# A hybrid decoder block on one core: the MLP's VectorE, ScalarE and TensorE instructions issued in the written order, and the sums of activations at places of their own

## The chip, the cores and the metric

One core of one Trainium2 chip runs the whole program. The time is the device time of one launch in microseconds (us), from an execution without the profiler; the median of several runs is compared. Engines are named as in the profile: PE is TensorE (PEld its weight loads), DVE is VectorE, ACT is ScalarE, POOL is GpSimd, SP issues most of the DMAs.

## The reference, cut to what matters

512 tokens with 16 meta tokens ahead of them pass through a mixer (a Mamba-2 part and an S5 part, one input and one output projection) and then through an MLP. All data are float32. The change touches the MLP and the step into it:

```python
m = _rmsnorm(h, g_mlp[layer]) @ w_up[layer]          # 512 x 1024 @ 1024 x 4096
h = h + jnp.square(jax.nn.relu(m)) @ w_down[layer]   # 512 x 4096 @ 4096 x 1024
return _rmsnorm(h, g_final)[:, N_META:]
```

## The kernel before

**Three matmuls for one.** Float32 operands are split into a high part (`whi`, `ah`: a cast to fp32r on ACT, line 1012) and a rest (`wlo`, `al`: the difference, on DVE, line 997), and each product is made as high x high, rest x high and high x rest.

**Seven products for eight.** Each matrix product of the MLP is done on 2 x 2 blocks with seven block products in place of eight (a Strassen-like scheme). So sums of blocks are needed on both sides, of weights and of tokens, and sums of products behind them.

**Quarters, groups, steps.** The 4096 hidden columns go in four quarters of 1024, each of two groups of 512. A quarter has 28 steps, numbered 0 to 27 within it and 0 to 111 over all (`for i in range(112)`, line 1394):

- Steps 0 to 13 are the up projection (`up`, line 1217): seven products P1 to P7 for each of the two groups, 24 matmuls of 128 x 256 each. In quarters 1 to 3 the order is P1, P5, P6, P2, P7, P3, P4 of group 0, then of group 1; quarter 0 has an order of its own (line 1153).
- Steps 14 to 27 are the down projection (`down`, line 1254): products n = 0 to 6 (`PRODUCTS`), each for group 0 and group 1, 12 matmuls of 128 x 512 each. The last product is done for both groups at once in step 27 (`last`).

**Taking over an up product** (lines 1236 to 1252). The products of a group go to three PSUM banks, X (P1, P6, P7, P4), Y (P2) and Z (P5, P3). P1, P5 and P6 are copied into the tile `r` by ACT. P2, P7 and P3 are added to or subtracted from what is in `r` by DVE, and ACT then applies relu and square (lines 1073 and 1074). P4 goes through relu and square on ACT alone. A bank that is used again must have been taken over first. The pool of these banks (tag `u`) has six.

**Weights.** `Cols` and `Rows` load blocks of `w_up` and `w_down` with SP (lines 1052 and 1091) and form sums of them: `s1` (two DVE additions, line 99), `s2` (one), `s4` (a DMA issued by POOL that adds while it writes, line 1009), and `t1`, `t2`, `t4` for the rows. The loads and the sums have due steps in the table `self.at`; `ahead(i)` does what is due at step i. In quarters 1 to 3, `s1` is due one step ahead of a group's first product, `s2` at that product, `s4` one later. `split(i + 2)` casts and splits the weights for the step after next (three buffers each for `whi` and `wlo`), and for down steps the operand of activations (two buffers for `ah` and `al`).

**Sums of activations** (`Sums`, line 1110). The down products need S1 = a11 - a10, S2 = -(S1) - a00, S3 = a00 - a10 and S4 = -(S2) - a01 of blocks of `r`. `Sums.get` computes each at the moment that its product is split: S1 and S2 in `split` of step 18, S3 of step 22, S4 of step 24, each over both groups.

**The order.** The program is recorded in the order in which it is written, and a scheduler then makes a queue for each engine. It goes by priority (the written order, moved ahead by `tc.high_priority(offset=AHEAD)`) among what its own estimate of the times holds to be ready, so an engine's queue can differ from the written order. In each round of the loop the written order is `ahead(i)`, `split(i + 2)`, then `run(i)` with the take-over. Within a queue an engine goes in order.

**The step into the MLP.** Tokens come in four tiles of 128. Tiles 0 and 1 are transposed and split during the end of the output projection (`first_blocks`). Tiles 2 and 3 are done by `late_tokens` (line 1379), written behind step 0 at high priority: `turned` transposes (PE) into two PSUM banks, DVE makes two differences (t1, t2), ACT and DVE split them into `opB`, and ACT copies the transposed blocks into `H`. In steps 4, 5 and 7 three more operands (`opC`) are made from `H`. `TOK` says which operand a product uses: P1 and P2 `opA`, P5 and P6 `opB`, P7, P3 and P4 `opC`.

**The end.** In the last quarter the finished parts of the output rows are normed as they come (`finish`, line 1307, after products n = 1, 4, 5, and `last_half`, `last_done`).

## Time and profile before

| | us |
|---|---|
| median of 3 runs | 819.64 (818.76 to 822.69) |
| the profiled execution | 819.08 |
| its span, first to last instruction | 817.4 |
| mean granted clock of PE | 0.991 |
| first MLP matmul, last MLP matmul | 472.36, 809.2 |

The mixer takes the first 472 us, the MLP the rest. By engine, over the stretch 740 to 770 us (up steps) PE is busy all 30.0 us, DVE 23.6, ACT 21.9; over 770 to 800 us (down steps) PE 28.6, DVE 29.7, ACT 18.8.

How to read it: a row of a timeline has the start, the duration, the engine, the line, the operation, output <- inputs, the shapes, how many instructions were merged, and in brackets how long the engine had been idle and what released it. A group of the page has, behind its count, busy time and mean duration in ns, then the idle time of its engine just before it. A DVE operation of 128 x 1024 takes 1.22 us, and the next one starts 1.14 us after it; matmuls overlap in the same way, so their rate is read from a run of many.

### The profile page before, as it was taken

What the parts mean: (1) busy time and instruction counts of PE and PEld (TensorE: products, weight loads), DVE (VectorE), ACT (ScalarE), POOL (GpSimd) and SP (SyncE); (2) the same over time, 40 slices, a digit from 0 to 9 for tenths busy, and PEclk for the clock granted to TensorE, in tenths of its full rate; (3) what the DMA queues carried; (4) which work ended last, traced back from release to release, by engine and by line L of the source; (5) the groups of instructions that cost most, each with busy time, mean ns of one, the idle gap of its engine ahead of it and who ended that gap; (6) DMA issues with size and microseconds to landing.
All of it is one profiled execution on the core that took longest, in us unless ns stands there. A gap on an engine that the chain in (4) does not pass through costs nothing. (4 is left out here: it accounts for less than half of the span.)

```text
span 817.4 us, 12922 instructions
## 1 busy us (share of the span) xinstructions
PE 774.6 (95%) x4943; PEld 682.0 (83%) x4943; DVE 625.9 (77%) x972; ACT 496.3 (61%) x782; POOL 75.5 (9%) x125
## 2 busy tenths in 40 slices
PE   6999899999999999989999989999999999999996
PEld 6999898998787778768888879878997899789975
DVE  4489798998785779769534588698679867987897
ACT  7578798988544753555123475654665466546665
POOL 3211000011000110010100000100010001000101
PEclk9999999999999999999999999999999999999998
DMA  9999575768664654344335028864485448654622
GB/s 242 194 232 217 113 167 138 172 141 190 144 154 133 163 131 132 104 125 160 123 103 186 21 78 244 192 155 156 129 181 155 156 130 181 180 159 112 117 51 104
DMA packets 129638, 121.90 MB, mean 149 GB/s; under 512 B 21836, under 2 KB 105720, under 8 KB 129576
## 3 DMA queue, kind: packets, MB, share of 16 engines
q1 hardware_dynamic: 121224, 90.66, 37.7%
q0 software_dynamic: 8352, 30.41, 20.4%
q8 instruction: 39, 0.64, 0.3%
q14 instruction: 23, 0.19, 0.1%
HBM read 83.76 MB, written 6.88 MB: 111 GB/s over the span
## 5 line engine op out<-in xcount | busy, mean ns | idle before, releaser
L997 DVE TENSOR_TENSOR wlo<-quad,whi 128x1024 fp32r<-128x1024 f32 x40 | 49.0, 1224 | 37.1 <-ACT whi L1012 34.5
L1232 PE MATMUL u<-opC,whi 128*128 128x256 f32 x384 | 71.5, 288 | 3.0 <-DVE r L99 2.0
L1012 ACT CAST whi<-quad 128x1024 fp32r<-128x1024 f32 x40 | 41.9, 1048 | 49.3 <-DMA quad<-raw 17.3
L1273 PE MATMUL acc<-whi,al 128*128 128x512 f32 x160 | 63.4, 396 | 3.7 <-DVE al L997 3.7
L1232 PEld LDWEIGHTS u<-opC,whi 128*128 128x128 f32 x384 | 60.6, 195 | 4.6 <-DVE r L99 2.6
L117 ACT CAST whi<-raw 128x1024 fp32r<-128x1024 f32 x31 | 32.3, 1043 | 52.6 <-PE acc L837 31.6
L118 DVE TENSOR_TENSOR wlo<-raw,whi 128x1024 fp32r<-128x1024 f32 x31 | 37.9, 1222 | 31.8 <-ACT whi L117 31.2
L1273 PE MATMUL acc<-whi,ah 128*128 128x512 f32 x160 | 59.6, 393 | 1.4 <-ACT ah L1012 1.4
L1273 PE MATMUL acc<-wlo,ah 128*128 128x512 f32 x160 | 60.3, 390 | 0.0
L139 PE MATMUL pxb<-xhi,whi 128*128 128x264 f32 x192 | 55.3, 288 | 1.6 <-ACT xcr L695 1.6
L139 PE MATMUL pxb<-xhi,wlo 128*128 128x264 f32 x192 | 55.8, 291 | 0.0
L139 PE MATMUL pxb<-xlo,whi 128*128 128x264 f32 x192 | 55.5, 289 | 0.0
L1232 PE MATMUL u<-opC,wlo 128*128 128x256 f32 x192 | 54.0, 286 | 0.0
L1012 ACT CAST whi<-bquad 128x1024 fp32r<-128x1024 f32 x34 | 35.7, 1049 | 30.0 <-PE acc L1273 20.8
L1232 PE MATMUL u<-opB,whi 128*128 128x256 f32 x256 | 48.6, 288 | 1.2 <-DVE opB L997 1.2
L1232 PE MATMUL u<-opA,whi 128*128 128x256 f32 x256 | 46.7, 280 | 0.2 <-ACT whi L1012 0.2
L997 DVE TENSOR_TENSOR wlo<-bquad,whi 128x1024 fp32r<-128x1024 f32 x34 | 41.5, 1221 | 3.2 <-ACT whi L1012 3.2
L1232 PEld LDWEIGHTS u<-opB,whi 128*128 128x128 f32 x256 | 40.8, 194 | 1.6 <-DVE opB L997 1.4
L1273 PEld LDWEIGHTS acc<-whi,al 128*128 128x128 f32 x160 | 30.0, 188 | 13.4 <-DVE al L997 7.5
L1232 PEld LDWEIGHTS u<-opA,whi 128*128 128x128 f32 x256 | 39.5, 188 | 0.6 <-ACT whi L1012 0.4
L1232 PE MATMUL u<-opB,wlo 128*128 128x256 f32 x128 | 37.1, 290 | 2.4 <-DVE wlo L997 2.4
L122 POOL DMA_DIRECT2D wlo<-raw x26 | 22.3, 856 | 179.2 <-ACT xcr L695 62.0
(435 smaller groups left out, 2429.0 us busy)
## 6 DMA issues: line engine op xcount, KB each, us to landing
raw<-in_w_in_dram SPq DMA_DIRECT2D x28, 512.0 KB, 4.2
wlo<-raw POOLq DMA_DIRECT2D x26, 512.0 KB, 5.2
raw<-in_w_up_dram SPq DMA_DIRECT2D x22, 512.0 KB, 4.2
raw<-in_w_glu_dram SPq DMA_DIRECT2D x16, 512.0 KB, 4.0
raw<-in_w_out_dram SPq DMA_DIRECT2D x16, 512.0 KB, 4.2
bquad<-in_w_down_dram SPq DMA_DIRECT2D x16, 512.0 KB, 3.6
quads<-in_w_down_dram SPq DMA_DIRECT2D x16, 512.0 KB, 4.4
bquad<-quads POOLq DMA_DIRECT2D x16, 512.0 KB, 5.1
```

Of the source, the lines that this page charges most:

```text
L117: A.copy(hi, raw)
L118: V.tensor_tensor(out=lo, in0=raw, in1=hi.bitcast(F32), op=ALU.subtract)
L122: G.dma_start(out=lo.bitcast(F32), in_=raw, accum_op=ALU.add)
L139: T.matmul(ps_out, lhsT=w[a][:, k, 0:m], rhs=x[b][:, k, tok], start=(n == 0), stop=(n == len(steps) - 1))
L997: V.tensor_tensor(out=out, in0=a, in1=b, op=ALU.subtract)
L1012: A.copy(hi, src)
L1232: T.matmul(pb[:, mm], lhsT=w[a][:, k, mm * P:(mm + 1) * P], rhs=x[:, b, k], start=(first and n == 0), stop=(n in (11, 23)), skip_group_che ...
L1273: T.matmul(banks[s], lhsT=at[x][:, g, j, s * P:(s + 1) * P], rhs=wt[y][:, j], start=(fresh and g == 0 and j == 0 and k == 0), stop=(g == 1 ...
```

## The change

It does four things.

1. `V`, `A` and `T` become wrappers (`InOrder`). While `on` is set, each instruction issued through a wrapper is tied behind the one issued before it on that engine, in order of issue and with no wait for its end. It is switched on for all three ahead of step 0; at step 107 it is switched off for VectorE and ScalarE. POOL and SP are not wrapped, and neither is anything written before step 0.
2. The sums of activations leave `Sums.get` and become due steps of their own: S1 and S2 of group 0 at step 8 (12 in quarter 0), of group 1 at step 15, S3 at 19, S4 at 20.
3. `late_tokens` is cut into `late_sums`, `late_split` and `late_copies`, no longer at high priority, and steps 0 to 3 are written out with these parts between them.
4. In these first steps the splits of weights for steps 2 to 5 are put between the parts, `s2` of the first group stands behind step 1, and `ahead(1)` stands with `ahead(3)` behind step 2.

```diff
+class InOrder:
+    def __init__(self, tc, engine):
+        self.tc, self.engine, self.on, self.last = tc, engine, False, None
+    def __getattr__(self, name):
+        f = getattr(self.engine, name)
+        def issue(*args, **kwargs):
+            r = f(*args, **kwargs)
+            if self.on:
+                if self.last is not None:
+                    self.tc.add_manual_dep(
+                        r.ins, self.last.name,
+                        mybir.DependencyInfo(mybir.DependencyClass.NoSync, mybir.DependencyReason.DATA),
+                        reason="in order")
+                self.last = r.ins
+            return r
+        return issue
...
-    V, A, G, T = nc.vector, nc.scalar, nc.gpsimd, nc.tensor
+    V, A, G, T = InOrder(tc, nc.vector), InOrder(tc, nc.scalar), nc.gpsimd, InOrder(tc, nc.tensor)
...
+        def first(self, g):
+            a = self.a
+            sub(self.s1[:, g], a[1, 1][:, g], a[1, 0][:, g])
+            neg_sub(self.s2[:, g], self.s1[:, g], a[0, 0][:, g])
+        def third(self):
+            sub(self.s1, self.a[0, 0], self.a[1, 0])
+        def fourth(self):
+            neg_sub2(self.s2, self.s2, self.a[0, 1])
         def get(self, m):
-            a = self.a
             if m in ("11", "12", "22"):
-                return a[int(m[0]) - 1, int(m[1]) - 1]
-            if m == "S2":
-                sub(self.s1, a[1, 1], a[1, 0])
-                neg_sub2(self.s2, self.s1, a[0, 0])
-            elif m == "S3":
-                sub(self.s1, a[0, 0], a[1, 0])
-            elif m == "S4":
-                neg_sub2(self.s2, self.s2, a[0, 1])
+                return self.a[int(m[0]) - 1, int(m[1]) - 1]
             return self.s1 if m in ("S1", "S3") else self.s2
...
+            self.add(12 if q == 0 else 8, self.sums_first)
+            self.add(15, lambda: self.sums.first(1))
+            self.add(19, lambda: self.sums.third())
+            self.add(20, lambda: self.sums.fourth())
...
+        def sums_first(self):
+            self.sums = Sums(self.rs)
+            self.sums.first(0)
...
-                if i == 14:
-                    self.sums = Sums(self.rs)
...
-    def late_tokens(t):
+    def late_sums(t):
+        c = slice((t - 2) * P, (t - 1) * P)
+        t1 = H[:, 0, 0, :, c]
+        src = [turned(t, k) for k in range(2)]
+        sub(t1, src[0], t1)
+        sub(t2[:, :, c], src[1], t1)
+        return src
+    def late_split(t, o):
+        c = slice((t - 2) * P, (t - 1) * P)
+        split_into(opB[:, o, 0, :, c], opB[:, o, 1, :, c], H[:, 0, 0, :, c] if o else t2[:, :, c])
+    def late_copies(t, src):
         c = slice((t - 2) * P, (t - 1) * P)
         for k in range(2):
...
+            A.copy(H[:, k, 1, :, c], src[k])
...
-    for i in range(112):
+    for e in (V, A, T):
+        e.on = True
+    def run(i):
+        quarters[i // 28].run(i % 28)
+    run(0)
+    src2 = late_sums(2)
+    split(2)
+    src3 = late_sums(3)
+    for t in late:
+        late_split(t, 1)
+    split(3)
+    run(1)
+    quarters[0].cols[0].s2()
+    late_copies(2, src2)
+    late_copies(3, src3)
+    for t in late:
+        late_split(t, 0)
+    split(4)
+    run(2)
+    for i in range(1, 4):
+        if i != 2:
+            ahead(i)
+    split(5)
+    run(3)
+    for i in range(4, 112):
...
-        if i > 0:
-            ahead(i)
+        if i == 107:
+            V.on = A.on = False
+        ahead(i)
         split(i + 2)
...
-        quarters[i // 28].run(i % 28)
-        if i == 0:
-            with tc.high_priority(offset=AHEAD):
-                for t in late:
-                    late_tokens(t)
+        run(i)
```

## The prediction

> **What bounds the kernel now.** I read the page, then what TensorE (PE) waits for in the MLP, then its clock there, then the rows of each engine in time.

> ```profile
> span 817.4 us, 12922 instructions
> PE 774.6 (95%) x4943; PEld 682.0 (83%) x4943; DVE 625.9 (77%) x972; ACT 496.3 (61%) x782; POOL 75.5 (9%) x125
> ```

> PE is the bound. The MLP begins at 472.4 us, so a change there can only gain what PE loses there:

> ```profile
> PE acc L1273 <- DVE al L997: 3.7, 6, 0.7
> PE u L1232 <- DVE wlo L997: 2.8, 2, 2.4
> PE u L1232 <- DVE r L99: 2.0, 1, 2.0
> PE acc L1273 <- ACT ah L1012: 1.4, 1, 1.4
> PE u L1232 <- DVE opB L997: 1.2, 1, 1.2
> PE u L1232 <- ACT whi L1012: 1.2, 4, 0.4
> ```

> That is 12.3 us. To it comes the clock after two of the gaps (second fence: a stretch, its length, PE busy, granted clock, DMA share, GB/s):

> ```profile
> 490.94 0.39 PE L1232 MATMUL u<-opB,wlo 128*128 128x256 f32 x1 [2.37 <-DVE wlo L997]
> 522.12 0.75 PE L1232 MATMUL u<-opC,whi 128*128 128x256 f32 x2 [1.95 <-DVE r L99]
> ```

> ```profile
> 492.00:494.00 2.00, 2.00 (x11) 0.50 0.67 129
> 494.00:496.00 2.00, 2.00 (x16) 0.78 0.98 137
> 522.00:524.00 2.00, 1.88 (x9) 0.55 0.34 66
> 524.00:526.00 2.00, 2.00 (x13) 0.60 1.05 197
> ```

> These four stretches lost 1.0, 0.44, 0.9 and 0.8, about 3.1 us, 1.6 for each gap. So 15.4 us, 1.9%, is the ceiling of a gain. [...]

> PE's steps without loss come from two rows of the chain that ended last:

> ```profile
> 728.94 40.07 PE u L1232 x336
> 781.83 21.60 PE acc L1273 x94
> ```

> 14 up steps take 40.07 us, 2.86 each; eight down steps 21.6, 2.70 each; the last one, of double length, 5.4. A quarter without loss is 40.1 + 12 x 2.70 + 5.4 = 77.9 us. Its first up steps show what it took:

> ```profile
> 647.58 0.40 PE L1232 MATMUL u<-opA,whi 128*128 128x256 f32 x2
> 728.78 0.40 PE L1232 MATMUL u<-opA,whi 128*128 128x256 f32 x2
> ```

> 81.2 us, so quarter 2 loses 3.3.

> **The order that the change takes away.** In an up step with a DVE take-over (P2, P7, P3), before, in quarter 1:

> ```profile
> 576.85 1.23 DVE L997 TENSOR_TENSOR wlo<-quad,whi 128x1024 fp32r<-128x1024 f32 x1 [2.72 <-ACT whi L1012]
> 577.99 0.68 DVE L997 TENSOR_TENSOR r<-u,r 128x512 f32<-128x512 f32 x1
> 578.59 1.22 DVE L997 TENSOR_TENSOR wlo<-raw,whi 128x1024 fp32r<-128x1024 f32 x1
> ```

> ```profile
> 577.48 1.05 ACT L1012 CAST whi<-raw 128x1024 fp32r<-128x1024 f32 x1 [0.19 <-PE u L1232]
> 578.71 0.63 ACT L1073 ACTIVATE r<-r 128x512 f32<-128x512 f32 x1 [0.17 <-DVE r L997]
> 579.37 0.63 ACT L1074 ACTIVATE r<-r 128x512 f32<-128x512 f32 x1
> ```

> ACT casts the weight of step 6 at 577.48, as soon as PE has freed its buffer, ahead of the relu and square of step 3; DVE can follow at 578.59. The written order has them the other way round: take-over of step i-1 (DVE), relu and square (ACT), cast of step i+2 (ACT), rest of step i+2 (DVE), take-over of step i (DVE). With ACT and DVE each held to that order it is one serial turn: 0.68 + 0.63 + 0.63 + 1.05 + 1.22 = 4.21 us, against 2.86 of PE. Three such steps follow each other in each group.

> **A steady quarter, by hand.** Times from PE's end of step 3, starts of a next DVE operation 1.14 after a 1.22 one. Sums of weights are late first: S += b01 is a DMA that cannot start before the rest of step 2:

> ```profile
> 571.08 4.59 DMA quad<-raw
> 591.77 5.24 DMA quad<-raw
> ```

> At the turn of a quarter DVE does the rest of step 1, two additions, S += b00, then the cast and rest of step 2: some 5.6 us behind PE's end of the last step; 4.6 of DMA, a cast and a rest make 12.6, where PE ends step 3 at 11.5. The take-over of P2 so starts 1.2 late. From there: P2 taken at 1.9, squared 3.2, weight 6 cast 4.25, its rest 5.5, P7 taken 6.15. P4 needs that bank at 5.7: 0.5 lost. Weight 7's rest 9.65, due at 8.8 + 0.5: 0.35 lost. P3 taken 10.3, two additions of the next group's sums to 12.6, weight 8's rest 13.85, due 12.55: 1.3. S += b00, cast, rest of weight 9 at 17.35, due 16.7: 0.65. Then the DMA of 5.24 and again cast, rest, take-over, relu2, cast, rest, take-over: P7 is out of its bank at 30.0, P4 of the second group wanted it at 28.55: 1.5. Two more turns stand before the rests of the first two down weights: about 0.8 and 2.0. Sum 7.1; with something for the next down steps, 7.5. Before lost 3.3 (among it gaps on al, which I count as gone: the earlier sums put the S2 operand in time). Net +4.2 in each of quarters 1 to 3: +12.5 us. Bounds: at -3.3 the turn costs nothing, at +6 each DMA lands 1 us later as well.

> **Startup.** Before, PE's first transposes go between the first matmuls, and ACT copies them out at once:

> ```profile
> 475.61 0.57 ACT L1390 COPY H<-pt 128x512 f32<-128x512 f32 x1
> 476.37 0.58 ACT L1390 COPY H<-pt 128x512 f32<-128x512 f32 x1 [0.19 <-DVE bquad L997]
> ```

> ```profile
> 474.98 0.75 DVE L872 SCALAR_TENSOR_TENSOR xs<-h_tok,rh,gains 128x512 f32<-128x512 f32 x1
> 475.65 0.68 DVE L997 TENSOR_TENSOR bquad<-pt,H 128x512 f32<-128x512 f32 x1
> 476.25 2.47 DVE L99 TENSOR_TENSOR quad<-quad,raw 128x1024 f32<-128x1024 f32 x2
> ```

> ```profile
> raw<-in_w_up_dram SPq DMA_DIRECT2D x22, 512.0 KB, 4.2
> ```

> Tag u has six banks: step 0, four transposed pieces, step 1. Step 2 needs a seventh. In the written order the copies stand behind step 1's relu and square, so the first bank to come free is step 1's, after DVE's take-over; ahead of that stand, from 475.7, s1 (2.3), four subtractions (2.4), two rests (2.3), two rests of opB (1.2): 484.9 with hand-overs. PE ends step 1 at 480.1 (472.4 + two steps + 2.0 of transposes): a gap of 4.8 us. PE cannot fill it: T is in order too. Later, the load for the second group's b10 waits for the rest of step 6 (497.5), lands 4.6 later (issue and 4.2), and s1 stands in front of every DVE operation: weight 8's rest at 505.8, due 503.3, 2.5 lost; then P7's take-over, t2, cast and rest of opC2, S += b00, cast, rest of weight 9: 513.4, due 508.6, 4.8 lost. Small waits at steps 4, 6 and 10: 2.2. Sum 14.3; up steps end at 472.4 + 40.1 + 2.0 + 14.3 = 528.8. Before, the chain's down steps begin at the end of the up steps:

> ```profile
> 526.75 4.56 PE acc L1273 x20
> ```

> So +2.0. The gaps of 4.8, 2.5 and 4.8 would each halve the clock for a while, at the 1.6 of the rows above; the first two are hidden in the next wait for DVE, the third in part: +1.0 (0 to 3). Down steps of quarter 0: the late rests of the first down weights cost 2.6, the two al gaps that go give 1.2 back: +1.3. Bounds of the startup: -4 if s1 stands before 474 and banks come free otherwise, +8 if loads come behind each other. SP and POOL are not held to an order; b.load(0,1) is written later (step 3 instead of 1), but step 5 needs it, and I cost it at nothing while SP issues it before 485; if SP takes it behind other loads it is 4.6 late.

> **Last quarter.** The first norm of the output rows now stands in DVE's queue:

> ```profile
> 781.68 0.63 ACT L1340 ACTIVATE os<-h_tok 128x512 f32<-128x512 f32 x1
> 782.22 0.19 ACT L1340 ACTIVATION_READ_ACCUMULATOR os<-h_tok 128x1 f32 x1
> ```

> ```profile
> 784.81 0.15 DVE L1341 TENSOR_SCALAR hst<-hst 128x1 f32<-128x1 f32 x1
> 784.87 0.69 DVE L1342 TENSOR_TENSOR os<-h_tok,last_gain 128x512 f32<-128x512 f32 x1
> ```

> ```profile
> 781.83 0.73 PE L1273 MATMUL acc<-whi,ah 128*128 128x512 f32 x2 [1.39 <-ACT ah L1012]
> ```

> Before, DVE did other work for 2.4 us between ACT's sum and L1341. In order, each of two rows takes 0.60 + 0.9 of waiting + 0.15 + 0.6 before the next; behind them wait al and the rest of step 20, for which PE waits. It costs 2 x 1.65 = 3.3 of pure delay, some 0.2 more with hand-overs: +3.5 (0 to 6). From step 107 on DVE and ACT are free: nothing.

> **The sum.** 2.0 + 1.0 + 1.3 + 12.5 + 3.5 = +20.3 us on the profiled execution's 819.08 (span 817.4 and 1.7 around it) gives 839.4. The median of three is 819.64, 0.56 above it: 840.0 us. No instruction is added or made longer (S1 and S2 of group 0 become two half-size operations, 0.1 us each more), so all of this is queueing.

> **The rivals.** *Faster.* The before order rests on the scheduler's estimates; an addition that waits for its load stands in front of take-overs (the 1.95 gap). If the written order has slack where I see turns, the al, ah and r gaps go: 3.7 + 1.4 + 2.0 = 7.1 us and a 1.6 clock loss, 810.4; with all gaps gone 804. For it: earlier sums need only 2.4 us of DVE in up steps. Against: 4.21 against 2.86. It decides at weight 8: if its rest lands within 11.7 us of the end of step 3 (hand: 13.85 with PE by then 0.85 late), quarters lose nothing. Chance 0.14.

> *Absorbed.* Turn and gain cancel: startup +2, quarters 0, norm 0, then 821; also the case that the edges bind little because the engine orders were close already. The rows at 577.48 and 578.71 speak against it. 0.13.

> *Deeper.* DVE blocked by loads that SP issues late: another 4.6 us in startup and 1.5 to 3 in each quarter: 855. For it: in-order DVE has nothing to do meanwhile. 0.07.

> **How the numbers follow.** Forecast 0.66, rivals 0.14, 0.13, 0.07. Half a per cent (815.5 to 823.7) is about what a measurement can tell. The forecast and the deeper case are slower; of the absorbed case 0.05 is. So slower 0.78, within 0.08, faster 0.14. Likeliest case alone: 828 to 852 (quarters +1.5 to +6, startup -2 to +6). With the absorbed case the range is 816 to 852, leaving out some 0.2.

> **What would show it.** Right: in the new profile ACT's casts follow L1074 in up steps, take-overs lie 4.2 us apart, PE waits for DVE wlo in u steps at the second group's P5 and P6 and for DVE r before P4, 6 to 8 us per quarter, over 83 us from quarter to quarter; one gap near 480 before the third up step of over 3 us; no al gap at step 18. Wrong: quarters of 80 us or less; casts that still stand ahead of relus; a startup whose up steps end before 524.

## The result, and the profile after

The kernel after takes 851.08 us (median of 4 runs, 850.88 to 852.41) against 819.2 for the kernel before; the ratio is 1.0385 with a 95% interval of 1.0352 to 1.0418. The forecast was 840.0 (816 to 852), slower at 0.78: the side is right, the time is 11 us short and lies at the range's edge. The profiled execution took 852.41 us.

The page's first rows, for the kernel after:

```profile
span 850.7 us, 12935 instructions
PE 787.5 (93%) x4943; PEld 688.2 (81%) x4943; DVE 629.0 (74%) x976; ACT 497.0 (58%) x782; POOL 74.8 (9%) x125
```

The span is 33.3 us longer, with DVE and ACT doing nearly the same work as before (629.0 and 497.0 us against 625.9 and 496.3). The time goes to waits, and to a halved clock of PE behind some of them (last section). What PE waits for in the MLP (us in total, times, longest; in this trace every instruction issued through a wrapper has line L63, so tiles tell them apart):

```profile
PE u L63 <- DVE r L63: 10.2, 7, 4.9
PE acc L63 <- DVE wlo L63: 5.5, 13, 0.6
PE u L63 <- DVE wlo L63: 5.4, 9, 0.8
PE acc L63 <- ACT whi L63: 5.0, 5, 1.2
PE u L63 <- ACT whi L63: 3.9, 2, 3.5
PE acc L63 <- DVE h_tok L63: 1.3, 2, 0.8
PE ybank L63 <- DVE wlo L63: 0.7, 3, 0.2
```

Waits of 12.3 us have become 32.0, now on take-overs (`r`), on rests (`wlo`) and on casts (`whi`), with 1.3 on `h_tok`; those on `al`, 3.7 us before, are gone. Where the time went is read from PE's first matmul of each quarter, such as these two of the kernel after:

```profile
576.40 0.40 PE L63 MATMUL u<-opA,whi 128*128 128x256 f32 x2
663.08 0.40 PE L63 MATMUL u<-opA,whi 128*128 128x256 f32 x2
```

86.7 us from one to the next, where the kernel before took 81.6. The same reading for every kernel of this study, in us (quarter 3 to the last matmul):

| kernel | first MLP matmul | quarter 0 | 1 | 2 | 3 | median |
|---|---|---|---|---|---|---|
| before | 472.36 | 93.65 | 81.57 | 81.20 | 80.42 | 819 to 821 |
| after | 474.61 | 101.79 | 86.68 | 86.54 | 93.28 | 851.08 |
| e1: sums' places alone | 476.41 | 94.17 | 81.42 | 80.59 | 82.71 | 823.35 |
| e2: order alone, old sums | 473.56 | 106.10 | 92.14 | 91.93 | 97.72 | 870.81 |
| e3: cast ahead of relu | 475.54 | 100.03 | 79.12 | 78.96 | 85.74 | 828.83 |
| e4: early copies | 472.60 | 100.78 | 87.30 | 86.50 | 93.33 | 850.04 |
| e5: VectorE's order alone | 473.77 | 96.55 | 80.19 | 80.40 | 84.58 | 825.50 |
| e6: ScalarE's order alone | 472.64 | 96.87 | 88.60 | 86.34 | 85.20 | 837.44 |
| e8: VectorE, ScalarE free from 98 | 474.10 | 100.74 | 87.41 | 86.47 | 92.05 | 850.11 |
| e9: order in 28 to 97, cast first | 474.29 | 93.82 | 78.84 | 78.92 | 80.42 | 816.76 |
| e10: TensorE free | 472.93 | 100.10 | 85.57 | 85.65 | 89.83 | 844.22 |
| e11: e9 from step 12 | | | | | | 813.84 |
| e12: e9 from step 8 | 474.64 | 91.34 | 78.87 | 79.09 | 80.52 | 814.42 |
| e13: e9 from step 3 | 474.92 | 95.72 | 79.11 | 79.15 | 82.17 | 818.87 |

e11 has no stages here: its profiled execution took 1531.65 us, unlike its other five (812.07 to 815.8).

So the 33.3 us are quarter 0 with 8.1, quarters 1 and 2 with 5.1 and 5.3, quarter 3 with 12.9, 2.25 ahead of the MLP, and 0.4 less behind it.

A steady quarter shows the turn that the prediction drew. DVE of the kernel after, up steps 3 to 5 of quarter 2:

```profile
676.49 0.68 DVE L63 TENSOR_TENSOR r<-u,r 128x512 f32<-128x512 f32 x1
679.47 1.23 DVE L63 TENSOR_TENSOR wlo<-raw,whi 128x1024 fp32r<-128x1024 f32 x1 [2.30 <-ACT whi L63]
680.61 0.68 DVE L63 TENSOR_TENSOR r<-u,r 128x512 f32<-128x512 f32 x1
683.59 1.22 DVE L63 TENSOR_TENSOR wlo<-raw,whi 128x1024 fp32r<-128x1024 f32 x1 [2.30 <-ACT whi L63]
684.74 0.68 DVE L63 TENSOR_TENSOR r<-u,r 128x512 f32<-128x512 f32 x1
```

and ACT in the same stretch:

```profile
677.21 1.29 ACT L63 ACTIVATE r<-r 128x512 f32<-128x512 f32 x2 [1.89 <-DVE r L63]
678.41 1.03 ACT L63 CAST whi<-raw 128x1024 fp32r<-128x1024 f32 x1
```

Each engine stands idle for the other in turn: 2.30 us of DVE for the cast, 1.89 of ACT for the take-over. Take-overs lie 4.12 and 4.13 us apart; the prediction had 4.21. What PE loses by it in quarter 2:

```profile
681.44 0.47 PE L63 MATMUL u<-opC,whi 128*128 128x256 f32 x2 [0.87 <-DVE r L63]
689.00 0.39 PE L63 MATMUL u<-opB,wlo 128*128 128x256 f32 x1 [0.76 <-DVE wlo L63]
692.61 0.38 PE L63 MATMUL u<-opB,wlo 128*128 128x256 f32 x1 [0.27 <-DVE wlo L63]
704.79 0.47 PE L63 MATMUL u<-opC,whi 128*128 128x256 f32 x2 [0.72 <-DVE r L63]
...
712.28 0.50 PE L63 MATMUL acc<-whi,ah 128*128 128x512 f32 x1 [0.96 <-ACT whi L63]
713.54 0.50 PE L63 MATMUL acc<-wlo,ah 128*128 128x512 f32 x1 [0.53 <-DVE wlo L63]
```

These are the places that the prediction named: P4 of group 0, the second group's P5 and P6, P4 of group 1, and the first down weights.

### The profile page after: what moved, and what is told of

Its sections match the earlier page's. It is cut to its first block, busy times and chain, and to the rows that moved or that the text cites. A ratio compares the mean times of both kernels' runs of the same rounds, so it can differ in the third digit from the quotient of the medians.

```text
span 850.7 us, 12935 instructions
## 1 busy us (share of the span) xinstructions
PE 787.5 (93%) x4943; PEld 688.2 (81%) x4943; DVE 629.0 (74%) x976; ACT 497.0 (58%) x782; POOL 74.8 (9%) x125
## 4 chain that ended last, share of the span: by engine, by line
PE 48%; DVE 18%; ACT 13%; DMA 11%; issue 8%; POOL 1%; SPq 1%; POOLq 0%; ACTq 0%; DVEq 0%
PE acc L63 19%; DVE wlo L63 5%; PE pu L63 4%; PE u L63 4%; ACT whi L63 4%; PE pz L63 3%; PE pg L63 3%; PE pv L63 3%; DMA quad<-raw 2%; DMA ab<-aD 2%; PE acct L63 2%; ACT r L63 2%; PE pxb L63 2%; PE pt L63 2%; DVE quad L63 2%
## 5 line engine op out<-in xcount | busy, mean ns | idle before, releaser
L63 ACT CAST whi<-raw 128x1024 fp32r<-128x1024 f32 x79 | 82.4, 1043 | 78.0 <-PE acc L63 36.6
L63 DVE TENSOR_TENSOR wlo<-raw,whi 128x1024 fp32r<-128x1024 f32 x53 | 64.8, 1223 | 54.4 <-ACT whi L63 53.9
L63 PE MATMUL acc<-wlo,ah 128*128 128x512 f32 (+1 forms) x200 | 79.1, 395 | 5.5 <-DVE wlo L63 5.5
L63 PE MATMUL acc<-whi,ah 128*128 128x512 f32 (+1 forms) x200 | 78.1, 391 | 6.3 <-ACT whi L63 5.0
L63 PE MATMUL acc<-whi,al 128*128 128x512 f32 (+1 forms) x200 | 77.3, 386 | 0.0
L63 PE MATMUL u<-opC,whi 128*128 128x256 f32 x384 | 70.4, 284 | 5.5 <-DVE r L63 5.3
L63 DVE TENSOR_TENSOR wlo<-quad,whi 128x1024 fp32r<-128x1024 f32 x40 | 48.9, 1223 | 34.1 <-ACT whi L63 34.1
L63 ACT CAST whi<-quad 128x1024 fp32r<-128x1024 f32 x40 | 41.9, 1050 | 45.7 <-DVE quad L63 19.7
L63 PEld LDWEIGHTS u<-opC,whi 128*128 128x128 f32 x384 | 59.6, 191 | 6.9 <-issue 6.6
L63 ACT ACTIVATE r<-r 128x512 f32<-128x512 f32 x56 | 35.4, 632 | 47.3 <-DVE r L63 46.2
L63 PE MATMUL pxb<-xhi,whi 128*128 128x264 f32 x192 | 55.7, 290 | 1.6 <-ACT xcr L63 1.6
L63 PE MATMUL pxb<-xhi,wlo 128*128 128x264 f32 x192 | 56.2, 293 | 0.0
L63 PE MATMUL pxb<-xlo,whi 128*128 128x264 f32 x192 | 56.0, 292 | 0.0
L63 PE MATMUL u<-opC,wlo 128*128 128x256 f32 x192 | 54.4, 283 | 0.8 <-DVE wlo L63 0.8
L63 PE MATMUL u<-opB,whi 128*128 128x256 f32 x256 | 49.4, 292 | 4.0 <-ACT whi L63 3.9
L63 PE MATMUL u<-opA,whi 128*128 128x256 f32 x256 | 48.2, 289 | 4.9 <-DVE r L63 4.9
L63 PEld LDWEIGHTS acc<-wlo,ah 128*128 128x128 f32 x200 | 38.2, 191 | 17.9 <-DVE wlo L63 10.7
L63 PEld LDWEIGHTS acc<-whi,ah 128*128 128x128 f32 x200 | 38.3, 191 | 15.5 <-ACT whi L63 7.1
L63 PEld LDWEIGHTS u<-opA,whi 128*128 128x128 f32 x256 | 41.2, 197 | 5.4 <-issue 5.1
L63 PEld LDWEIGHTS u<-opB,whi 128*128 128x128 f32 x256 | 40.8, 195 | 5.4 <-ACT whi L63 5.0
L63 PEld LDWEIGHTS acc<-whi,al 128*128 128x128 f32 x200 | 38.3, 191 | 7.4
L63 DVE TENSOR_TENSOR wlo<-bquad,whi 128x1024 fp32r<-128x1024 f32 x34 | 40.8, 1221 | 2.9 <-ACT whi L63 2.5
## 6 DMA issues: line engine op xcount, KB each, us to landing
raw<-in_w_in_dram SPq DMA_DIRECT2D x28, 512.0 KB, 4.2
wlo<-raw POOLq DMA_DIRECT2D x26, 512.0 KB, 5.2
raw<-in_w_up_dram SPq DMA_DIRECT2D x22, 512.0 KB, 3.7
raw<-in_w_glu_dram SPq DMA_DIRECT2D x16, 512.0 KB, 4.0
raw<-in_w_out_dram SPq DMA_DIRECT2D x16, 512.0 KB, 4.0
bquad<-in_w_down_dram SPq DMA_DIRECT2D x16, 512.0 KB, 4.9
quads<-in_w_down_dram SPq DMA_DIRECT2D x16, 512.0 KB, 4.6
bquad<-quads POOLq DMA_DIRECT2D x16, 512.0 KB, 4.9
```

What stands on the lines that cost most here:

```text
L63: r = f(*args, **kwargs)
```

## The experiments

The theory: written order on DVE and ACT closes a loop (take-over, relu and square, cast, rest, take-over) that is longer than PE's step, and the startup and the last quarter lose by other queueing of the same kind. The main rival: the new places of the sums, or DVE's load, cost the time.

**e1 and e2, the two halves.** e1 is the kernel before with the new places of the sums only; e2 is the kernel after with them back in `Sums.get`:

```diff
 e1, against after
-    V, A, G, T = InOrder(tc, nc.vector), InOrder(tc, nc.scalar), nc.gpsimd, InOrder(tc, nc.tensor)
+    V, A, G, T = nc.vector, nc.scalar, nc.gpsimd, nc.tensor
 (and steps 0 to 3 and late_tokens as before)
 e2, against after
-            self.add(12 if q == 0 else 8, self.sums_first)
-            self.add(15, lambda: self.sums.first(1))
-            self.add(19, lambda: self.sums.third())
-            self.add(20, lambda: self.sums.fourth())
 (and S1 to S4 computed in Sums.get as before)
```

> The kernel before, with the sums of activations at their new places (first group's part in the up projection, the others at steps 15, 19, 20) and no written order on any engine. My theory, that the loss of 32 us comes from the order alone: the sums no longer stand between the last square and step 16, so some of the before kernel's 3.3 us of gaps per quarter go and the time is 814 to 819 us, nothing above 821. Rival, that the sums placed among the ups cost VectorE time which delays take-overs of banks: 823 to 835 us. If the sums' places are the whole loss, 850 us.

> The kernel after, with the sums back where the kernel before makes them (when step 16's and later operands are asked for) and the written order kept. My theory, the order alone costs the time: 851 to 858 us, the sums then standing in VectorE's queue in front of the down steps' first weights, so a gap of 1 to 1.5 us per quarter at step 16 to 18 on top. Rival, the new places of the sums are what costs: 820 to 835 us.

Measured: e1 823.35 us, ratio to before 1.0042 (1.0020 to 1.0064); e2 870.81, 1.0621 (1.0587 to 1.0655). The order is what costs, and by far; e2 holds the rewritten steps 0 to 3 as well, and no run has these without an order, so what they cost by themselves stays open. But both numbers missed my windows; e1's lies at the lower edge of the rival's. The sums' places alone are a small loss, not the small gain I expected, and it sits in quarter 3 (82.71 against 80.42). And within the written order the new places are worth 20 us: the down steps of e2 take 47.3 us in each quarter 0 to 2 where the kernel after takes 41.8 to 42.6. e2's DVE at the first split that needs S2:

```profile
728.91 1.29 DVE L63 SCALAR_TENSOR_TENSOR last_gain<-S,r 128x512 f32<-128x512 f32 x2
731.37 1.23 DVE L63 TENSOR_TENSOR al<-last_gain,ah 128x1024 fp32r<-128x1024 f32 x1 [1.17 <-ACT ah L63]
```

The sums, ACT's cast of them, `al` and the weight's rest now stand in one row, and PE waits 1.59 and 0.64 us at its end, with 3.4 us of half clock behind (matmuls 0.43 us apart in place of 0.23, from 734.1 to 737.5). Whether an instruction's place costs anything depends on whether the queue may move it: +3 us in a free order, -20 in a written one.

**e3, the loop opened at one place.** The relu and square of P2, P7 and P3 are issued behind the next weight's cast:

```diff
     def split_w(src):
...
-        split_into(hi, lo, src)
+        A.copy(hi, src)
+        flush_relu2()
+        sub(lo, src, hi.bitcast(F32))
...
-                relu2(r[0, 0], r[0, 0])
+                put_off_relu2(r[0, 0], r[0, 0])
 (P7 and P3 likewise; the first two down weights are also split ahead of their activations)
```

> The kernel after, with the relu and square of P2, P7 and P3 written behind the next weight's cast instead of ahead of it, from step 4 on. My theory, the turn of VectorE and ScalarE (take-over 0.68, relu and square 0.63 + 0.63, cast 1.05 then rest 1.22 in one chain of 4.21 us against 2.86 us of TensorE per up step): the cast is off the chain, the chain falls to about 3.0 us, take-overs stand about 3 us apart, each quarter falls from 86.6 us to 80 to 82, and the time to 829 to 836 us. Rival, the quarters lose to VectorE's own load in the written order and not to the turn: 848 to 853 us.

Measured: 828.83 us, quarters 1 and 2 at 79.12 and 78.96. Same engines in order, same load, and 7.6 us of a quarter go. Up to step 11 only the swap acts, and there the kernel after's losses of 3.4 us (at P4 of group 0 and the rests of weights 7 to 9) are gone, which settles the turn. For P4 of group 1 and the first down weights the swap and the other edit are not told apart. e3's DVE in the same steps:

```profile
668.05 0.68 DVE L63 TENSOR_TENSOR r<-u,r 128x512 f32<-128x512 f32 x1
668.65 1.22 DVE L63 TENSOR_TENSOR wlo<-raw,whi 128x1024 fp32r<-128x1024 f32 x1
669.79 0.68 DVE L63 TENSOR_TENSOR r<-u,r 128x512 f32<-128x512 f32 x1
671.04 1.23 DVE L63 TENSOR_TENSOR wlo<-raw,whi 128x1024 fp32r<-128x1024 f32 x1 [0.57 <-ACT whi L63]
672.22 0.69 DVE L63 TENSOR_TENSOR r<-u,r 128x512 f32<-128x512 f32 x1
```

The rest follows the take-over with no wait or with one of 0.57 us, and the next take-overs come 1.74 and 2.43 us after the last one instead of 4.12. The quarters are even 2.2 to 2.5 us shorter than in the kernel before. The rival, DVE's own load, is out.

**e4, the startup's gap.** `late_copies(2, src2)` and `late_copies(3, src3)` move up, right behind their `late_sums`.

> The kernel after, with the copies of the two late token tiles (they free the turned banks) written right behind the sums that read the same banks, and so ahead of the splits of weights 2 to 4 and of the other token splits on ScalarE. My theory, TensorE's 4.94 us gap near 487 us is a wait for a bank whose reader is queued behind those: the gap falls to 1 us or less, the halved clock of 486 to 494 us goes with it (1 to 2 us more), and the time to 844 to 848 us. Rival, the gap belongs to the rests of the up weights on VectorE: unchanged within 1 us, 850 to 852 us.

Measured: 850.04 us, ratio 1.0391 where the kernel after has 1.0385. The gap is gone, so its cause was right, but the time is the rival's; 3.4 of the 6.8 us at half clock stay as well (matmuls 0.21 us apart in place of 0.12, from 488.2 to 491.6). e4's PE in its place:

```profile
481.06 0.50 PE L63 MATMUL u<-opA,whi 128*128 128x256 f32 x2 [0.94 <-ACT whi L63]
482.32 0.38 PE L63 MATMUL u<-opA,wlo 128*128 128x256 f32 x1 [0.76 <-DVE wlo L63]
486.31 0.50 PE L63 MATMUL u<-opB,whi 128*128 128x256 f32 x2 [1.16 <-ACT whi L63]
487.57 0.39 PE L63 MATMUL u<-opB,wlo 128*128 128x256 f32 x1 [0.76 <-DVE wlo L63]
```

3.62 us of waits for casts and rests that now stand behind the copies, in place of 4.94 for the bank.

**e5 and e6, one engine alone.** `for e in (V, A, T)` becomes `(V,)` and `(A,)`.

> The kernel after, with only VectorE kept in the written order; ScalarE and TensorE are left to the scheduler. My theory, the turn of 4.1 us closes only if take-over, relu and square, cast and rest stand in written order on both engines: with ScalarE free its casts run ahead, the rests find them done, and the second and third quarter take 80.5 to 83 us where the kernel after has 86.6. The startup may keep its loss, so the time is 824 to 840 us. Rival, VectorE's order alone loses the quarters' time: 86 us per quarter and 846 to 853 us.

> The kernel after, with only ScalarE kept in the written order. My theory (the turn needs both engines): the take-over of the next bank need not stand behind the rest, so the chain has no way back, the quarters take 80.5 to 83.5 us, and the time is 822 to 840 us. Rival, ScalarE's order alone (cast behind relu and square) loses the quarters' time: 86 us per quarter and 846 to 853 us.

Measured: e5 825.5 us with quarters of 80.2 and 80.4, a little under the 80.5 to 83 that I expected: with DVE alone in order the loop is open. e6 837.44 us: the time fell into my window, the quarters (88.6 and 86.3) did not, so e6 does not speak for the theory. The loop is open in it, but another wait took its place, in e6's DVE:

```profile
675.83 2.48 DVE L63 TENSOR_TENSOR quad<-quad,raw 128x1024 f32<-128x1024 f32 x2 [3.62 <-DMA quad<-in_w_up_dram]
678.23 0.68 DVE L63 TENSOR_TENSOR r<-u,r 128x512 f32<-128x512 f32 x1
```

The free scheduler put two additions that wait 3.62 us for a load in front of a take-over, and PE waits 1.83 us for `r` behind them; in the down steps of that quarter it waits 2.18 us for `al`.

**e8 and e10, the last quarter and TensorE.** e8: `if i == 107:` becomes `if i == 98:`. e10: `for e in (V, A):`, TensorE is free throughout.

> The kernel after, with the written order of VectorE and ScalarE ended at step 98 (the fourth quarter's first down step) and not at 107; TensorE keeps it. My theory, the fourth quarter's down steps lose 48.7 - 41.9 = 6.9 us against the other quarters' because the norm's steps stand in VectorE's queue in front of the rests: with the order ended the wait near 815 us (1.19 + 0.64) and those of the last step (0.50 + 0.52 + 0.77) go in part, the down steps take 41 to 45 us, and the time is 843 to 848 us. Rival, the norm is late whatever the order: 850 to 853 us.

> The kernel after, with TensorE left to the scheduler; VectorE and ScalarE keep the written order. My theory, TensorE's order by itself costs where it could have done something else: in the kernel before it did the first down step (3.0 us) ahead of the last up step of the first quarter, and in the last step it changes between banks while VectorE reads one (0.52 + 0.77 us of waits for h_tok after, none before): 844 to 848 us, quarters 2 and 3 unchanged at 86.5 to 86.7 us. Rival, TensorE's order costs nothing, since the operands are late in any order of it: 849.5 to 852 us.

Measured: e8 850.11 us, the rival's time; its last down steps take 46.7 us in place of 48.7, so the order of DVE and ACT there is 2 us of the loss and not the 4 to 8 that I expected. e10 844.22 us, in the window, with quarter 3 at 89.83 in place of 93.28; quarters 1 and 2 gain 1 us each, where I had expected none. In the kernel after PE waited in the last step like this:

```profile
836.32 0.39 PE L63 MATMUL acc<-wlo,ah 128*128 128x256 f32 x1 [0.50 <-DVE wlo L63]
837.58 0.38 PE L63 MATMUL acc<-whi,ah 128*128 128x256 f32 x1 [0.52 <-DVE h_tok L63]
841.48 0.39 PE L63 MATMUL acc<-whi,ah 128*128 128x256 f32 x1 [0.77 <-DVE h_tok L63]
```

None of the three is in e10. As the last step is written, the second half of a bank comes right behind the first, which DVE is still reading (0.42 us from 837.10, 0.41 from 841.01); a free PE need not keep to that. That e8, which frees DVE and ACT but not PE, keeps both waits for `h_tok` (0.52 and 0.76) says the same.

**e9 to e13, the order only where it pays.** e9 is the kernel before with the sums' new places, the order with the cast first (both edits of e3), and

```diff
+        if i in (28, 98):
+            V.on = A.on = T.on = late_relu[0] = i == 28
```

e11, e12 and e13 put 12, 8 and 3 for 28.

> The kernel before, with the sums at their new places, all three engines in the written order only in steps 28 to 97, and there the relu and square of P2, P7 and P3 behind the next weight's cast; first quarter and last down steps as the scheduler orders them. My theory, the written order costs time in the turn, the startup and the last down steps, and is worth about 2 us per quarter where the turn is opened (79.1 and 79.0 us per quarter with the cast first, 81.6 and 81.2 in the kernel before): from the MLP's start to its last matmul 94.2 + 79.1 + 79.0 + 40.1 + 40.4 to 41.4 = 333 to 334 us against 336.8 before, time 813 to 819 us. Rival, what is saved in the middle comes back where the order is switched on and off: 819 to 824 us.

> The kernel of 816.8 us (sums at new places; steps 28 to 97 in the written order with the cast first), with this order beginning at step 12 of the first quarter. My theory, its wait of 2.61 us ahead of the first quarter's last up step comes from additions that wait for a load and stand, by the scheduler's estimate, in front of a take-over; in the written order the take-over goes first, the halved clock behind the gap goes too (1.6 us), and the down steps fall from 40.4 to about 39 us: 811.5 to 815 us. Rival, the load is late and holds the written order up too: 816 to 819 us.

> As the one from step 12, with the order beginning at step 8. My theory, the startup loses in the written order while sums wait for the late loads of the second group's weights (gaps of 3.45 and 0.47 us near step 9 with the cast first everywhere), so this one is 1 to 4 us slower than from step 12: 813 to 818 us. Rival, those gaps come from the token operands written at steps 4 to 7 and are gone by step 8: equal to the one from step 12 within 1 us.

> As the kernel whose written order (cast first) begins at step 8, with the order beginning at step 3: VectorE then has the rest of weight 5 ahead of the token operands of steps 4 and 5, for which TensorE waited 2.34 us near 493 us. My theory, that gap goes and its halved clock (1.6 us) with it, but the operand of step 7 now stands in front of weight 9's sum, which brings back the gap of 3.5 us near 514 us that all kernels with a written startup have (515.08 in the kernel after): no net gain, 813 to 816 us. Rival, the gap near 514 us belongs to the banks and copies of steps 0 to 2, which stay free here: 809 to 812 us.

Measured, against before in the same rounds: e9 816.76 us, 0.9962 (0.9941 to 0.9983); e11 813.84, 0.9917 (0.9886 to 0.9947); e12 814.42, 0.9924 (0.9896 to 0.9952); e13 818.87, 0.9988 (0.9967 to 1.0008). e9 and e11 came as expected. e12's time lies in both of its windows, and the 0.6 us to e11 is within the spread; its trace speaks for the rival, since of the gaps of 3.45 and 0.47 us only one of 0.76 is there. So the late waits of the written startup are set by steps 3 to 7. e13, whose time lies in neither window, shows how. PE's wait of 2.34 us falls to 0.21, and the one near weight 9 is back; e13's DVE there:

```profile
505.38 1.21 DVE L63 TENSOR_TENSOR bquad<-H,bquad 128x1024 f32<-128x1024 f32 x1
507.70 1.23 DVE L63 TENSOR_TENSOR opC<-bquad,opC 128x1024 fp32r<-128x1024 f32 x1 [1.11 <-ACT opC L63]
508.85 1.22 DVE L63 TENSOR_TENSOR quad<-quad,bquad 128x1024 f32<-128x1024 f32 x1
511.23 1.23 DVE L63 TENSOR_TENSOR wlo<-quad,whi 128x1024 fp32r<-128x1024 f32 x1 [1.17 <-ACT whi L63]
```

The operand of step 7 (505.38, 507.70) stands in front of weight 9's sum (508.85) and rest (511.23), with two waits for ACT between. The direction was expected, the size not: 4.4 us in quarter 0 against e12. e11 and e12 beat both kernels, the kernel before by 0.8%, which is little but clear of noise.

## Why the prediction was right in kind and short in size

**The turn: right.** 4.21 us was forecast, 4.12 measured, casts stand behind the relus, and e3 takes it away.

**A steady quarter: +4.2 forecast, +5.1 and +5.3 measured.** The mechanism was right, and so was the size at most places. What a wait costs PE is read from the starts of its matmuls, which lie 0.12 us apart in up steps and 0.23 in down steps when nothing is waited for. So measured in quarters 1 and 2, weight 7's rest cost 0.3 us (0.35 forecast), weight 8 1.3 (1.3), weight 9 0.7 (0.65), P4 of group 1 1.5 and 1.0 (1.5), the first two down weights 2.7 (2.8). Two terms were too small: P4 of group 0, 1.0 and 1.1 (0.5), and the waits at steps 16 and 18, together 0.9, for which 0.4 was allowed. The profile's brackets understate all this: they sum to 5.3 us in quarter 1, and the loss against 77.9 is 8.8.

**The startup: +2.0, +1.0 and +1.3 forecast, +8.1 measured.** This term failed, and not by its queues, which were drawn well. The bank gap was forecast with 4.8 us and is there with 4.94 (first row below); weight 9 was forecast with 4.8 and is there with 3.50 and 0.76; weight 8, forecast with 2.5, came out at 0.41 and 0.76. PE of the kernel after, with its first down matmul last:

```profile
487.07 0.77 PE L63 MATMUL u<-opA,whi 128*128 128x256 f32 x2 [4.94 <-DVE r L63]
515.08 0.50 PE L63 MATMUL u<-opB,whi 128*128 128x256 f32 x2 [3.50 <-ACT whi L63]
516.34 0.38 PE L63 MATMUL u<-opB,wlo 128*128 128x256 f32 x1 [0.76 <-DVE wlo L63]
533.80 0.39 PE L63 MATMUL acc<-whi,ah 128*128 128x512 f32 x1
```

The step that failed first is the clock. Its loss was put at 1.0 us, the first two gaps' share "hidden in the next wait for DVE"; half clock takes 4.6 us of these up steps (last section), and the waits came out only 1.8 us shorter than forecast. The up steps take 59.2 us, where the forecast had 56.4 and the 1.0. The second is the comparison in "Before, the chain's down steps begin at the end of the up steps". The kernel before had by then done four of the twelve matmuls of a down step (first to second row), and then waited:

```profile
519.08 0.40 PE L1273 MATMUL acc<-whi,ah 128*128 128x512 f32 x1
519.77 0.40 PE L1273 MATMUL acc<-whi,al 128*128 128x512 f32 x1
522.12 0.75 PE L1232 MATMUL u<-opC,whi 128*128 128x256 f32 x2 [1.95 <-DVE r L99]
526.59 0.40 PE L1273 MATMUL acc<-wlo,ah 128*128 128x512 f32 x1
```

The four matmuls are 0.9 us, so its up steps cost 53.3 us and not 54.4 (the 3.0 us that e10's expectation gives a whole down step here are mostly the wait). The change cost 5.9 us in the up steps. The down steps of this quarter, +1.3 forecast, take 42.6 us against 40.3: +2.3, of which 1.7 is half clock. That PE "cannot fill" the bank gap because it is in order was no reason: with PE free (e10) the gap is 4.93.

**The last quarter: +3.5 on top forecast, 7.7 in all; 12.9 measured.** The norm does stand in DVE's queue, with two waits for ACT, and PE waits behind it:

```profile
811.62 0.15 DVE L63 TENSOR_SCALAR hst<-hst 128x1 f32<-128x1 f32 x1 [0.79 <-ACT os L63]
813.76 0.15 DVE L63 TENSOR_SCALAR hst<-hst 128x1 f32<-128x1 f32 x1 [0.79 <-ACT os L63]
815.66 0.49 PE L63 MATMUL acc<-whi,ah 128*128 128x512 f32 x1 [1.19 <-ACT whi L63]
817.12 0.79 PE L63 MATMUL acc<-wlo,ah 128*128 128x512 f32 x1 [0.64 <-DVE wlo L63]
```

By the starts of matmuls these two waits cost 2.4 us, less than the 3.5. Three things were left out. "From step 107 on DVE and ACT are free: nothing" overlooked that TensorE is not: the three waits of the last step cost 2.3 us, and e10 loses them. Half clock behind the norm's waits adds 1.7. And the net of 4.2 takes off 3.3 us that the kernel before lost in quarter 2; in this quarter it lost 1.8, since its up steps took 40.07 us and its one wait is the 1.39 at the norm. With the steady part's shortfall this makes up the difference to within 0.3 us.

**Ahead of the MLP: 0 forecast, +2.25 measured.** Up to the MLP the queues of all the kernels in the table that have stages hold the same instructions in the same order, yet they reach it between 472.36 and 476.41 us. So 2.25 us is within the spread of one execution and not shown to be an effect of the change.

**The rivals and the range.** *Faster* fell with the turn: weight 8 was late. But e3 shows that a written order can be the shorter one, 79.0 us a quarter against 81.4, if the loop is open. *Absorbed*, at 821, fell with the quarters, which lost 5 us each and not nothing. *Deeper*, at 855, came nearest in time, yet not by its mechanism: only one load is waited for in the startup's DVE queue (1.97 us at 505.01), and the steady quarters wait for none. That 851.08 still lies below 852 is in part luck: the startup came out at its upper bound (+8), the last quarter above its own (some 7.7 on top, for 0 to 6), and all three parts were short on the same side.

## What to carry to other kernels

If the queues of two engines are fixed by hand, follow one unit of work from engine to engine until it meets its successor, add up that loop, and compare it with the step of the engine that bounds: here a relu and square issued behind a cast, with the small edit beside it, was worth 22 us. Fix the order where the work is periodic and its waits are known, and leave it to the scheduler where loads land late or the work ends; and when stages of two kernels are compared by their end times, first see that the same work has been done by then.

## What the hardware showed that was not expected

```profile
486.00:488.00 2.00, 0.93 (x4) 0.96 (x5) 2.00 (x3) 1.01 (x2) 0.00 (x0) 0.50 0.00 0
...
492.00:494.00 2.00, 2.00 (x16) 2.00 (x16) 1.25 (x2) 1.60 (x3) 0.28 (x1) 0.79 0.03 8
516.00:518.00 2.00, 1.66 (x9) 1.66 (x10) 0.89 (x2) 1.05 (x2) 0.85 (x1) 0.68 1.02 381
540.00:542.00 2.00, 2.00 (x7) 1.59 (x7) 1.43 (x2) 2.00 (x3) 0.86 (x1) 0.66 0.69 131
```

From 486 on it is 0.50 in every slice to 492; a mean of 0.79 is half clock until 492.84; 0.68 and 0.66 are half clock from 516.72 and from 540.64. Read in slices of half a us, the piece behind 817 runs from 817.10 to 820.51, 3.41 us. The edges are 23.88 and 23.92 us apart, seven times 3.41 each. The first piece lasts 6.8 us; the gap of 4.94 ends 1.1 us into it, so it costs 2.9 us of work. The others last 3.4 and cost 1.7 each; with one behind 817 the MLP loses 8.0 us to the clock, against 3.4 before (the prediction's 3.1 left out the half clock ahead of 492). A gap of one length need not cost the same: in e8 the same gap of 4.94 was followed by 3.4 us at half clock (0.61 in 486 to 488, 0.53 in 488 to 490, then 1.00) and not 6.8. Short waits have half clock behind them too: after those of 0.98 and 0.53 us in quarter 0 (ending at 538.50 and 539.76) comes the piece that starts at 540.64. The same pair in quarter 1, 0.96 and 0.53 us (625.78 and 627.04), cost no clock: it is 1.00 in every slice from 622 to 632. By an estimate of mine, counted on from the edge at 540.64 in steps of 3.41, the 25th step ends at 625.9, between the two; that this is why they differ was not shown.
